# Weight transfers of 2 MB with rows of 16 KB for the two mixtures of a two-block layer stack

## The chip, the cores and the metric

The kernel runs on one core of a Trainium2 chip. The metric is the device time of one execution in microseconds (us). PE is the matrix engine, with its weight loads (PEld) listed apart; DVE and ACT are the vector and scalar engines, POOL is GpSimd, and SP is the engine whose queue issues the weight transfers. A transfer is carried out by 16 DMA engines: each moves the rows of eight partitions, and a row arrives as one packet. The time to tell apart from no change is about 0.2%.

## The reference

All is float32, for 256 tokens of width 1024. A first block (gated linear attention, three groups of dilated attention, a gated projection) ends in a mixture of 32 experts with hidden width 512, and every token goes to two of them. A second block runs two layers of mixing; the first has a dense feed-forward, the second a mixture of 8 experts with hidden width 2816, again two of them for each token. What matters here is the product of an expert:

```
def expert_block(args):                       # first mixture
    xb, e = args
    return (silu(xb @ w_gate[e]) * (xb @ w_up[e])) @ w_down[e]
...
for e in range(N_EXPERTS_2):                  # second mixture
    out = out + gate[..., e:e + 1] * swiglu(x, w1[e], w3[e], w2[e])
```

The weights of the first mixture are 192 MB, those of the second 264 MB. Every weight is read once.

## The kernel before

The program runs nine phases in a row: `b1` (first block), `moe1` (first mixture), `mix0`, `ffn0`, `ple0`, `mix1`, `ffn1` (second mixture, method `moe2`), `ple1` and `fin`. Weights come through one stream (`Stream`, L236 to 275) in the order of a plan that `Kern.plan` writes (L525). Each entry of the plan is a tile of 128 partitions by 2048 float32, which is 1 MB in rows of 8 KB.

A ring of three such tiles serves all phases (`RING`, L17). A phase may widen it by a pool of its own (`WIDE`, L23): 13 more tiles for `moe1`, opened already near the end of `b1`, and 6 more for `ffn1`, opened when that phase starts. `fill` (L255) issues the next entries as long as a tile is free: one of the wide pool if the entry belongs to the phase that opened it, else one of the ring. `get` (L268) hands the next tile to the consumer and gives back the one handed out before. In the program, then, the transfer of entry k+16 in `moe1`, and of entry k+9 in `ffn1`, waits until the readers of entry k are done. All these transfers are issued from SP's queue at L264, and they complete on eight semaphores in turn, so that a transfer also waits for the eighth before it to have landed.

In `moe1` (`experts1`, L1183) the loop over 8 groups of four experts has 8 steps for gate and up and 4 steps for down. A step takes two tiles, that is 2 MB, and runs eight products, four experts beside each other in strips of 32 columns of PE.

In `ffn1` (`moe2`, L1894) there are two halves of four experts. Each half has 11 groups of 8 steps (gate and up), then two rounds of 22 steps (down). A step (`tiles`, L1918) takes one tile of 1 MB: eight products read it directly; ACT copies three 512-column pieces of it, chosen at run time, into a buffer `fw` (two of these buffers, `FLEX`), and six smaller products read that.

In each mixture, after its first part of products, a branch tests whether an expert has overflowed its places; its body (`overflow`, L976) reads weights straight from memory by small transfers and is skipped for the inputs here.

Of the kernel before, what the change touches and what calls it, by code (L numbers as in the profile page):

```python
# [7 lines left out]
F32 = mybir.dt.float32  # L8
# [11 lines left out]
DIL = ((128, 1), (512, 4), (2048, 16))  # L20
NEG = -1e30

WIDE = {"b1": 0, "moe1": 13, "mix0": 0, "mix1": 0, "ffn0": 2, "ffn1": 6, "ple0": 4, "ple1": 4, "fin": 0}  # L23

SPLIT = 4
CAP1, CAP2 = 32, 64
# [3 lines left out]
ROUTED = {"moe1": ("wr", 36), "ffn1": ("wr2", 8)}  # L30
# [91 lines left out]
def prep(I):  # L122
    I = {k: np.asarray(v) for k, v in I.items()}
    A = {}
# [22 lines left out]
    w = I["w_in"][0]  # L147
# [15 lines left out]
    g = I["w_gate"][0].reshape(8, 4, 8, 128, 512).transpose(0, 2, 3, 1, 4)  # L163
    u = I["w_up"][0].reshape(8, 4, 8, 128, 512).transpose(0, 2, 3, 1, 4)
# [8 lines left out]
    for l in range(2):  # L173
        w = I["w_in_2"][l]
        rb, cb = 512, 1536
        q = cb + qperm
# [10 lines left out]
        w = I["w_out_2"][l][np.concatenate([rows_of[m][128 * j:128 * j + 128] for m, j in MIXED])]  # L187
        wo.append(np.stack([_kt(w[c:c + 512], 4) for c in (0, 512)]))
        w = I["ple_gate_w_2"][l]
# [19 lines left out]
    A["f13"] = w13(I["ffn_w1_2"], I["ffn_w3_2"])[0]  # L209
    A["f2"] = w2(I["ffn_w2_2"])[0]  # L210
    g, u = [I[n][0].reshape(2, 4, 8, 128, 11, 2, 4, 32).transpose(0, 4, 2, 3, 1, 6, 5, 7) for n in ("moe_w1_2", "moe_w3_2")]
    A["m13"] = np.stack([g, u], -3).reshape(2, 11, 8, 128, 4, 512)
    A["m2"] = I["moe_w2_2"][0].reshape(2, 4, 22, 128, 2, 512).transpose(0, 4, 2, 3, 1, 5)
    A = {k: np.ascontiguousarray(v) for k, v in A.items()}
    return A, dict(c0=o0, c1=o1, c2=o2, pv=opv, rows=orow, sm1=osm1, sm2=osm2)

# [2 lines left out]
class Bank:  # L219


    def __init__(self, k, t):
        self.k, self.t, self.q = k, t, set()
# [12 lines left out]
class Stream:  # L236

    def __init__(self, k, plan, base):  # L240
        self.k, self.plan, self.i, self.issued, self.tiles = k, plan, 0, 0, []
        self.pools, self.free, self.phase, self.last = [base], [RING], None, None

    def widen(self, pool, n, phase):
# [10 lines left out]
    def fill(self):  # L255
        while self.issued < len(self.plan):
            ph, src = self.plan[self.issued]
            c = [j for j in range(len(self.pools)) if self.free[j] and (j == 0 or ph == self.phase)]
            if not c:
                return  # L260
            j = c[-1]
            self.free[j] -= 1
            t = self.pools[j].tile([128, 2048], F32, name="w")
            self.k.nc.sync.dma_start(t[:, :src.shape[-1]], src)  # L264
            self.tiles.append((j, t))
            self.issued += 1
# [11 lines left out]
class Kern:  # L278
# [244 lines left out]


    def plan(self):  # L525
        A, p = self.A, []
        half = lambda ap: [ap[:, i * (ap.shape[-1] // 2):(i + 1) * (ap.shape[-1] // 2)] for i in range(2)]
        for ph in self.phases:
            l = int(ph[-1]) if ph[-1].isdigit() else 0
            q = []  # L530
            if ph == "b1":
                q += [A["wgv"]] + [A["wgh"][i] for i in range(4)] + [A["wdh"][i] for i in range(12)]
                q += [A["wb1"][i] for i in range(8)]
            if ph == "moe1":
                for g in range(8):
                    q += [A["wgu"][8 * g + k] for k in range(8)] + [A["wdn"][4 * g + k] for k in range(4)]
            if ph == f"mix{l}":
                q += [A["wz"][l, i] for i in range(4)] + [A[n][l] for n in ("wc", "wz5", "wz6")] + [A["wo"][l, i] for i in range(2)]
            if ph == "ffn0":
                for j in range(11):  # L540
                    q.append(A["f13"][j])
                    if j and j % 2 == 0:
                        q.append(A["f2"][:, (j // 2 - 1) * 4096:(j // 2) * 4096])
                q.append(A["f2"][:, 20480:])
            if ph == f"ple{l}":
                q += [A["wpp"][l]] + [A["wpg"][l, i] for i in range(2)]
            p += [(ph, h) for ap in q for h in half(ap)]
            if ph == "ffn1":
                for c in range(2):
                    p += [(ph, A["m13"][c, j, k].rearrange("p e d -> p (e d)")) for j in range(11) for k in range(8)]  # L550
                    p += [(ph, A["m2"][c, i, k].rearrange("p e d -> p (e d)")) for i in range(2) for k in range(22)]
        return p

    def run(self):
        tc, nc, A = self.tc, self.nc, self.A
        with ExitStack() as ctx:
            pool = lambda name, bufs=1, **kw: ctx.enter_context(tc.tile_pool(name=name, bufs=bufs, **kw))
            self.keep = pool("keep")
            ring = pool("ring", RING)
# [10 lines left out]
                setattr(self, n, self.keep.tile(list(A[n].shape), F32, name=n))  # L570
                q.dma_start(getattr(self, n), A[n])
            self.p = self.keep.tile([128, 2, S], F32, name="p")
            self.W = Stream(self, self.plan(), ring)
            self.W.fill()
            split = lambda pool, dt=F32R: [pool.tile([128, 8, S], dt, name="raw" + c, tag="raw" + c, bufs=1) for c in "hl"]
            self.split = lambda dt: split(self.keep, dt)
# [16 lines left out]
            def widen(ph):  # L593
                if WIDE.get(ph) and ph not in wider:
                    wider.add(ph)
                    pool = self.room.enter_context(tc.tile_pool(reuse_waits="tile", name="ring" + ph, bufs=WIDE[ph]))
                    self.W.widen(pool, WIDE[ph], ph)
            for i, ph in enumerate(self.phases):
# [12 lines left out]
                with self.room as c:  # L611
# [12 lines left out]
                    else:  # L624
                        self.final(x)
                if WIDE[ph]:
                    self.W.narrow()
# [1266 lines left out]
    def moe2(self, x):  # L1894
# [13 lines left out]
        with tc.tile_pool(reuse_waits="tile", name="m2", bufs=1) as pool:  # L1908
# [21 lines left out]
            def first_products(c, also):  # L1930
                g = [self.bank() for _ in range(3)]
                for k in range(8):
                    also(k)
                    tiles(g, [v[:, k] for v, _ in xg[c]], self.W.get().rearrange("p (e d) -> p e d", e=4), c)
                return g
            with tc.tile_pool(reuse_waits="tile", name="m2r", bufs=1) as rt:
# [86 lines left out]
                f = {}  # L2023
# [22 lines left out]
                        self.tick()  # L2046
                g0 = first_products(0, during)
                self.drain()
            m13 = self.A["m13"].rearrange("q j k p e d -> q j k p e d")
            m2 = self.A["m2"].rearrange("q f (j c) p e d -> q f j c p e d", c=2)  # L2050

            def units(first, unit):
                with tc.For_i(0, 2, 1) as q:
# [4 lines left out]
            one = lambda i: bass.ds(i, 1)  # L2058
            with tc.tile_pool(reuse_waits="tile", name="m2e", bufs=1) as work:
# [8 lines left out]
                def flush():  # L2068
                    while later:
                        later.pop(0)()  # L2070

                for c in range(2):
                    for j in range(11):
                        g = g0 if c == j == 0 else first_products(c, lambda k: flush() if k == 2 else None)
                        ts = []
                        for r in range(3):
                            t = work.tile([128, 256], F32, name="ft", bufs=4)
                            gu = g[r].t.rearrange("p (q a d) -> p q a d", a=2, d=64)
                            t4 = t.rearrange("p (q d) -> p q d", q=4)
                            for q, u in [(slice(0, 4), r)] if r < 2 else [(slice(b, b + 1), 2 + of_block[b]) for b in range(3)]:  # L2080
                                u = rsl[:, 5 * c + u:5 * c + u + 1]
                                self.act(t4[:, q], gu[:, q, 0], AF.Silu, scale=u)
                                nc.vector.scalar_tensor_tensor(t4[:, q], gu[:, q, 1], u, t4[:, q], op0=ALU.mult, op1=ALU.mult)
                            ts.append(t)

                        def post(j=j, ts=ts):

                            for r in range(3):
                                for s in range(4):
                                    for q in range(4 if r < 2 else 3):  # L2090
                                        i, f = place(s, q) if r == 2 else (0, q)
                                        o = 128 * r + 32 * (i if r == 2 else s)
                                        nc.vector.transpose(hT[32 * f:32 * f + 32, 2 * j:2 * j + 2, o:o + 32],  # L2093
                                                            ts[r][32 * s:32 * s + 32, 64 * q:64 * q + 64].rearrange(
                                                                "p (i d) -> p i d", i=2))
                        later.append(post)
                        if c == 0 and j == 5:
                            self.overflow(pool, x, ("g_ffn1", xs, lambda: None), rk, *f["over"], E, units,
                                          lambda i, k: m13[one(i[0]), one(i[1]), k, :, i[2]].rearrange("o u p d -> (o u p) d"),
                                          lambda i, c, f: m2[one(i[0]), f, one(i[1]), c, :, i[2]].rearrange("o u p d -> (o u p) d"),  # L2100
                                          lambda v: v.rearrange("p (q a i d) -> p q a i d", q=4, a=2, i=2))
                    if c:

# [1 line left out]
                    for d in range(2):  # L2105
                        g = [self.bank() for _ in range(3)]
                        for k in range(22):
                            w = self.W.get().rearrange("p (e d) -> p e d", e=4)
# [64 lines left out]
```

## Time and profile before

| | us |
|---|---|
| median of 3 runs | 2163.77 |
| lowest and highest run | 2163.45, 2166.29 |
| the profiled execution, its own time | 2167.51 |
| its span, to which all rows refer | 2165.9 |
| PE busy | 2016.7 (93%) |
| ACT busy | 1080.2 (50%) |
| DVE busy | 1060.6 (49%) |
| queue of the weights (q1), share of 16 engines | 71.1% |

The rows come from one profiled execution, which took 3.7 us more than the median. Times in the rows are us from the start of the span. In the page's 40 slices one slice is 54.1 us; a digit is a busy share in tenths. PE counts as busy while a product is in its pipeline, so its share does not tell whether it works at its peak. An fp32 product stands in the trace as two records.

### The profile page before, as it was taken

The page shows a single profiled execution, that of the slowest core. Times are in us where ns is not written, and L with a number is a line of the kernel's source. Part 1 is how long each engine was busy: PE and PEld are TensorE (multiplying, and loading weights), DVE is VectorE, ACT ScalarE, POOL GpSimd, SP SyncE. Part 2 cuts the span into 40 slices and gives each one's busy share as a digit, 9 for nine tenths or more (in the row PEclk, how much of TensorE's full clock was granted, in tenths as well). Part 3 has the DMA queues.
Part 4 walks back from the last instruction along what each step waited for, and adds up shares of the span by engine and source line. Part 5 has one row for each costly group of instructions (what it writes and reads, how often), then busy time and mean ns, then how long its engine had stood idle before and what let it go on. Part 6 is the DMA issues. An engine that isn't in the chain of part 4 may idle for free. (4 is left out here: it accounts for less than half of the span.)

```text
span 2165.9 us, 44126 instructions
## 1 busy us (share of the span) xinstructions
PE 2016.7 (93%) x17740; PEld 1461.7 (67%) x17740; DVE 1060.6 (49%) x2809; ACT 1080.2 (50%) x2178; POOL 18.7 (1%) x29
## 2 busy tenths in 40 slices
PE   7999998787877779999999999999899999999997
PEld 6999994222222248879999888866566756666746
DVE  5787653100100037777666787536655115566115
ACT  5566642000000025456456735457677777777775
POOL 0000000000000010000000100000000000000000
PEclk9999999899999999999999999889999999999998
DMA  5344597999999983316555331449999999999981
GB/s 179 120 146 149 175 376 305 418 420 420 419 420 420 419 343 109 109 61 216 179 193 191 114 128 52 175 159 396 399 410 418 416 405 407 418 418 417 418 351 47
DMA packets 88665, 613.73 MB, mean 283 GB/s; under 512 B 9879, under 2 KB 12071, under 8 KB 18560
## 3 DMA queue, kind: packets, MB, share of 16 engines
q1 hardware_dynamic: 86272, 604.74, 71.1%
q0 software_dynamic: 1344, 5.10, 0.7%
q8 instruction: 143, 2.34, 0.4%
q10 hardware_dynamic: 832, 0.94, 0.1%
q14 instruction: 74, 0.61, 0.1%
HBM read 609.69 MB, written 1.05 MB: 282 GB/s over the span
## 5 line engine op out<-in xcount | busy, mean ns | idle before, releaser
L314 ACT COPY fw<-w 128x512 f32 x792 | 439.0, 617 | 137.3 <-ACT fw L314 91.9
L341 ACT CAST wh<-w 128x512 fp32r<-128x512 f32 (+2 forms) x500 | 289.8, 585 | 293.8 <-PE ps L230 247.1
L342 DVE TENSOR_TENSOR wl<-w,wh 128x512 fp32r<-128x512 f32 (+2 forms) x500 | 317.9, 646 | 169.9 <-ACT wh L341 161.8
L230 PE MATMUL ps<-w,hT 128*32 128x512 f32 x1920 | 311.0, 597 | 31.4 <-DMA w<-wdn 26.0
L230 PE MATMUL ps<-rawh,wh 128*128 128x256 f32 x960 | 277.4, 289 | 1.1 <-ACT rawh L341 1.1
L230 PE MATMUL ps<-rawl,wh 128*128 128x256 f32 x960 | 271.0, 282 | 0.5 <-DVE rawl L342 0.5
L230 PE MATMUL ps<-rawh,wl 128*128 128x256 f32 x960 | 270.5, 282 | 0.0
L230 PE MATMUL ps<-fw,xg 128*32 128x384 f32 (+2 forms) x2112 | 252.8, 382 | 0.0
L230 PE MATMUL ps<-w,xg 128*32 128x512 f32 x1024 | 199.5, 600 | 43.2 <-DMA w<-wgu 43.0
L2093 DVE STREAM_TRANSPOSE hT<-ft 32x64 f32<-32x64 f32 x968 | 228.3, 236 | 16.3 <-DVEq L985 0.7
L230 PE MATMUL ps<-w,rawh 128*32 128x512 f32 x1408 | 206.2, 607 | 6.4 <-issue 6.4
L230 PE MATMUL ps<-w,rawl 128*32 128x512 f32 x1408 | 211.7, 593 | 0.0
L230 PEld LDWEIGHTS ps<-w,hT 128*32 128x32 f32 x1920 | 116.8, 110 | 135.6 <-DMA w<-wdn 64.0
L230 PEld LDWEIGHTS ps<-fw,xg 128*32 128x32 f32 x2112 | 137.8, 110 | 83.0 <-issue 24.0
L230 PEld LDWEIGHTS ps<-rawh,wh 128*128 128x128 f32 x960 | 181.8, 190 | 5.1 <-ACT rawh L341 1.6
L230 PEld LDWEIGHTS ps<-rawl,wh 128*128 128x128 f32 x960 | 181.9, 190 | 1.9 <-DVE rawl L342 0.7
L230 PEld LDWEIGHTS ps<-rawh,wl 128*128 128x128 f32 x960 | 181.9, 189 | 1.5 <-issue 0.9
L230 PEld LDWEIGHTS ps<-w,xg 128*32 128x32 f32 x1024 | 42.1, 109 | 185.7 <-DMA w<-wgu 111.7
L230 PEld LDWEIGHTS ps<-w,rawl 128*32 128x32 f32 x1408 | 105.2, 110 | 34.4 <-issue 0.9
L230 PE MATMUL ps<-hh,wh 128*128 128x256 f32 x416 | 124.4, 300 | 0.1
L230 PE MATMUL ps<-fw,hT 128*32 128x128 f32 (+2 forms) x1056 | 121.1, 380 | 0.5 <-ACT fw L314 0.3
L230 PE MATMUL ps<-hh,wl 128*128 128x256 f32 x416 | 116.2, 281 | 0.2 <-DVE wl L342 0.2
(520 smaller groups left out, 2983.7 us busy)
## 6 DMA issues: line engine op xcount, KB each, us to landing
w<-m SPq DMA_DIRECT2D x264, 1024.0 KB, 10.7
w<-wgu SPq DMA_DIRECT2D x128, 1024.0 KB, 19.9
w<-wdn SPq DMA_DIRECT2D x64, 1024.0 KB, 19.9
w<-f SPq DMA_DIRECT2D x32, 1024.0 KB, 5.1
w<-wz SPq DMA_DIRECT2D x20, 1024.0 KB, 5.5
w<-wdh SPq DMA_DIRECT2D x24, 768.0 KB, 4.3
w<-wb SPq DMA_DIRECT2D x16, 1024.0 KB, 5.6
w<-wo SPq DMA_DIRECT2D x8, 1024.0 KB, 5.1
```

The source lines that it names most:

```text
L230: return self.k.nc.tensor.matmul(out, lhsT, rhs, start=new, stop=stop, skip_group_check=True, **kw)
L314: self.nc.scalar.copy(out, in_)
L341: self.nc.scalar.copy(h, src)
L342: self.nc.vector.tensor_sub(l, src, h.bitcast(F32))
L2093: nc.vector.transpose(hT[32 * f:32 * f + 32, 2 * j:2 * j + 2, o:o + 32], ts[r][32 * s:32 * s + 32, 64 * q:64 * q + 64].rearrange("p (i d) ...
```

## The change

The two mixtures' weights are laid out in memory so that one transfer brings 2 MB in rows of 16 KB, and `WIDE` has 6 tiles of 2 MB for `moe1` and 3 for `ffn1`, in place of 13 and 6 of 1 MB. `plan` keeps entries of 1 MB, in pairs, and beside them a table `whole` with each pair's full source. `fill` takes a pair in one transfer when a wide tile is free. If none is free but two of the ring's tiles are, the pair goes there as two transfers of 1 MB in rows of 8 KB, as before. The first half of a wide tile gives nothing back when it has been read; the second half gives back the whole tile. The products, their operands and the small transfers of the overflow body compute the same from the new layout.

```
-WIDE = {"b1": 0, "moe1": 13, "mix0": 0, "mix1": 0, "ffn0": 2, "ffn1": 6, "ple0": 4, "ple1": 4, "fin": 0}
+WIDE = {"b1": 0, "moe1": 6, "mix0": 0, "mix1": 0, "ffn0": 2, "ffn1": 3, "ple0": 4, "ple1": 4, "fin": 0}
...
-    A["m13"] = np.stack([g, u], -3).reshape(2, 11, 8, 128, 4, 512)
-    A["m2"] = I["moe_w2_2"][0].reshape(2, 4, 22, 128, 2, 512).transpose(0, 4, 2, 3, 1, 5)
+    A["m13"] = np.stack([g, u], -3).reshape(2, 11, 4, 2, 128, 4, 512).transpose(0, 1, 2, 4, 3, 5, 6)
+    A["m2"] = I["moe_w2_2"][0].reshape(2, 4, 11, 2, 128, 2, 512).transpose(0, 5, 2, 4, 3, 1, 6)
...
     def fill(self):
         while self.issued < len(self.plan):
             ph, src = self.plan[self.issued]
-            c = [j for j in range(len(self.pools)) if self.free[j] and (j == 0 or ph == self.phase)]
-            if not c:
+            wide = len(self.pools) > 1 and self.free[1] and ph == self.phase
+            two = ph in ROUTED and not self.issued % 2
+            if two and wide:
+                self.free[1] -= 1
+                t = self.pools[1].tile([128, 4096], F32, name="w")
+                self.k.nc.sync.dma_start(t, self.whole[self.issued])
+                self.tiles += [(None, t[:, :2048]), (1, t[:, 2048:])]
+                self.issued += 2
+                continue
+            j = 1 if wide and ph not in ROUTED else 0
+            if self.free[j] < 1 + (two and j == 0):
                 return
-            j = c[-1]
             self.free[j] -= 1
...
             if ph == "ffn1":
                 for c in range(2):
-                    p += [(ph, A["m13"][c, j, k].rearrange("p e d -> p (e d)")) for j in range(11) for k in range(8)]
-                    p += [(ph, A["m2"][c, i, k].rearrange("p e d -> p (e d)")) for i in range(2) for k in range(22)]
-        return p
+                    q += [A["m13"][c, j, k].rearrange("p k e d -> p (k e d)") for j in range(11) for k in range(4)]
+                    q += [A["m2"][c, i, k].rearrange("p k e d -> p (k e d)") for i in range(2) for k in range(11)]
+            for ap in q:
+                if ph in ROUTED:
+                    whole[len(p)] = ap
+                p += [(ph, h) for h in half(ap)]
+        return p, whole
```

Two places show the order of SP's queue, in which each row is a kind of transfer with its tile's shape (128x2048 is 1 MB, 128x4096 is 2 MB). The first is the end of `b1` up to the branch of `moe1`; `wb` are the last weights of `b1`, `wgu` and `wdn` those of the mixture. Before:

```order
L264 DMA w<-wgu 128x2048
L264 DMA w<-wb 128x2048 x2
L264 DMA w<-wgu 128x2048 x3
L264 DMA w<-wb 128x2048
L264 DMA w<-wgu 128x2048 x10
L264 DMA w<-wdn 128x2048 x8
L264 DMA w<-wgu 128x2048 x15
L984 TENSOR_LOAD fi
```

After:

```order
L265 DMA w<-wgu 128x4096
L274 DMA w<-wb 128x2048 x2
L265 DMA w<-wgu 128x4096
L274 DMA w<-wb 128x2048
L265 DMA w<-wgu 128x4096 x3
L274 DMA w<-wgu 128x2048 x3
L265 DMA w<-wgu 128x4096
L265 DMA w<-wdn 128x4096 x4
L265 DMA w<-wgu 128x4096
L274 DMA w<-wgu 128x2048
L265 DMA w<-wgu 128x4096 x4
L997 TENSOR_LOAD fi
```

Before the first product of the mixture 16 MB can be on their way (13 wide tiles and the ring), and 23 MB follow ahead of the branch; now it is six wide tiles and the ring's three, 15 MB, and 21 MB follow.

The second place is SP's queue in `ffn1`, where before 51 and then 213 transfers of 1 MB of `m` stand in a row, each behind the readers of the ninth before it. Now, from the phase's start:

```order
L274 DMA w<-m 128x2048 x3
L265 DMA w<-m 128x4096 x3
L274 DMA w<-m 128x2048 x2
L265 DMA w<-m 128x4096 x3
L274 DMA w<-m 128x2048 x2
L265 DMA w<-m 128x4096 x3
```

Three transfers of 2 MB alternate with two of 1 MB, so a wide tile comes round every 8 MB. In the whole program 83 transfers of 2 MB and 26 of 1 MB carry the first mixture, 99 and 66 the second.

## Rows read from the trace of the kernel before

**Rows 1.** The page's 40 slices: PE, granted clock, DMA engines, GB/s.
```profile
PE   7999998787877779999999999999899999999997
PEclk9999999899999999999999999889999999999998
DMA  5344597999999983316555331449999999999981
GB/s 179 120 146 149 175 376 305 418 420 420 419 420 420 419 343 109 109 61 216 179 193 191 114 128 52 175 159 396 399 410 418 416 405 407 418 418 417 418 351 47
```
**Rows 2.** Who waited for whom, whole run, engine PE: total us, times, longest.
```profile
PE ps L230 <- DMA w<-wgu: 43.0, 71, 1.6
PE ps L230 <- DMA w<-wdn: 26.0, 39, 2.3
```
**Rows 3.** Stretches: length, busy us (records) of PE, PEld, DVE, ACT, POOL; clock; DMA share; GB/s.
```profile
440.00:780.00 340.00, 270.16 (x1263) 73.61 (x1261) 25.20 (x40) 14.56 (x24) 0.00 (x0) 1.00 1.01 420
1800.00:2040.00 240.00, 239.85 (x2753) 165.89 (x2749) 127.85 (x523) 179.33 (x349) 0.00 (x0) 1.00 1.01 418
```
**Rows 4.** PE's timeline, late in moe1: start, length, operation, count, idle before.
```profile
755.60 1.91 PE L230 MATMUL ps<-w,xg 128*32 128x512 f32 x8 [0.59 <-DMA w<-wgu]
...
768.07 1.91 PE L230 MATMUL ps<-w,xg 128*32 128x512 f32 x8 [0.58 <-DMA w<-wgu]
```
**Rows 5.** ACT's timeline in ffn1, behind the branch and late in the second half.
```profile
1571.56 1.66 ACT L314 COPY fw<-w 128x512 f32 x3 [0.70 <-ACT fw L314]
1573.92 1.66 ACT L314 COPY fw<-w 128x512 f32 x3 [0.70 <-ACT fw L314]
...
2036.47 1.66 ACT L314 COPY fw<-w 128x512 f32 x3 [0.72 <-PE ps L230]
2038.98 1.66 ACT L314 COPY fw<-w 128x512 f32 x3 [0.84 <-DMA w<-m]
2041.46 1.66 ACT L314 COPY fw<-w 128x512 f32 x3 [0.82 <-DMA w<-m]
```
**Rows 6.** L264's transfers issued from 1586 to 1600, us from issue to landing.
```profile
DMA to landing us min/median/max: 7.8/8.4/11.4
```
**Rows 7.** The same from 1676 to 1696.
```profile
DMA to landing us min/median/max: 11.8/12.8/15.1
```
**Rows 8.** The same from 1784 to 1800, and from 2005 to 2025.
```profile
DMA to landing us min/median/max: 6.6/7.3/8.6
...
DMA to landing us min/median/max: 13.7/14.5/17.3
```
**Rows 9.** DMA view, 1151.29 to 1151.91: 60 packets of 4 KB and one semaphore's.
```profile
DMA packets 61, 0.25 MB, mean 396 GB/s; under 512 B 1, under 2 KB 1, under 8 KB 61
q1 hardware_dynamic: 61, 0.25, 96.5%
```
**Rows 10.** DMA view, 117.53 to 119.02: packets of 6 KB alone.
```profile
q1 hardware_dynamic: 97, 0.60, 95.2%
```
**Rows 11.** DMA view, 1380.58 to 1382.56: packets of 8 KB alone.
```profile
q1 hardware_dynamic: 103, 0.84, 100.5%
```
**Rows 12.** DMA view, 1372.56 to 1372.86: semaphore packets alone.
```profile
q1 hardware_dynamic: 15, 0.00, 2.8%
```
**Rows 13.** SP's queue as moe1 begins: start, length of the run of issues, count.
```profile
300.68 16.14 SPq L264 DMA_DIRECT2D w<-wgu  x10
343.17 0.80 SPq L264 DMA_DIRECT2D w<-wdn  x2
```
**Rows 14.** PE's timeline behind the branch of moe1.
```profile
387.44 3.75 PE L230 MATMUL ps<-pw,ysg 128*128 128x256 f32 x8 [6.75 <-issue]
```
**Rows 15.** DMA view, 2125 to 2127: one 16 KB packet of the instruction queue.
```profile
q8 instruction: 1, 0.02, 2.8%
```

More of the change, by code (lines that the diff above doesn't have):

```diff
@@ L236, with __init__ @@
 class Stream:
-    def __init__(self, k, plan, base):
-        self.k, self.plan, self.i, self.issued, self.tiles = k, plan, 0, 0, []
+    def __init__(self, k, plan, whole, base):
+        self.k, self.plan, self.whole, self.i, self.issued, self.tiles = k, plan, whole, 0, 0, []
         self.pools, self.free, self.phase, self.last = [base], [RING], None, None
@@ L525, in plan @@
     def plan(self):
-        A, p = self.A, []
+        A, p, whole = self.A, [], {}
         half = lambda ap: [ap[:, i * (ap.shape[-1] // 2):(i + 1) * (ap.shape[-1] // 2)] for i in range(2)]
@@ L546, in plan @@
                 q += [A["wpp"][l]] + [A["wpg"][l, i] for i in range(2)]
-            p += [(ph, h) for ap in q for h in half(ap)]
             if ph == "ffn1":
                 for c in range(2):
-                    p += [(ph, A["m13"][c, j, k].rearrange("p e d -> p (e d)")) for j in range(11) for k in range(8)]
-                    p += [(ph, A["m2"][c, i, k].rearrange("p e d -> p (e d)")) for i in range(2) for k in range(22)]
-        return p
+                    q += [A["m13"][c, j, k].rearrange("p k e d -> p (k e d)") for j in range(11) for k in range(4)]
[5 more added lines that the diff above has]
+        return p, whole
     def run(self):
@@ L572, in run @@
             self.p = self.keep.tile([128, 2, S], F32, name="p")
-            self.W = Stream(self, self.plan(), ring)
+            self.W = Stream(self, *self.plan(), ring)
             self.W.fill()
@@ L2048, in moe2 @@
                 self.drain()
-            m13 = self.A["m13"].rearrange("q j k p e d -> q j k p e d")
-            m2 = self.A["m2"].rearrange("q f (j c) p e d -> q f j c p e d", c=2)
+            m13, m2 = self.A["m13"], self.A["m2"]
             def units(first, unit):
@@ L2098, in moe2 @@
                             self.overflow(pool, x, ("g_ffn1", xs, lambda: None), rk, *f["over"], E, units,
-                                          lambda i, k: m13[one(i[0]), one(i[1]), k, :, i[2]].rearrange("o u p d -> (o u p) d"),
-                                          lambda i, c, f: m2[one(i[0]), f, one(i[1]), c, :, i[2]].rearrange("o u p d -> (o u p) d"),
+                                          lambda i, k: m13[one(i[0]), one(i[1]), k // 2, :, k % 2, i[2]].rearrange("o u p d -> (o u p) d"),
+                                          lambda i, c, f: m2[one(i[0]), f, one(i[1]), :, c, i[2]].rearrange("o u p d -> (o u p) d"),
                                           lambda v: v.rearrange("p (q a i d) -> p q a i d", q=4, a=2, i=2))
```

## The prediction

> **What bounds the kernel now.** Read the page's slices first [rows 1]. Two long plateaus show the DMA engines at 9 of 10 and about 420 GB/s: one from the seventh to the fourteenth slice, the first mixture, and one from the twenty-seventh to the thirty-eighth, the second. Outside them the weights' queue has air, and the change touches no other transfer. Then read who waits inside each plateau.
>
> In the first mixture PE waits for weights: 71 times for `wgu` and 39 times for `wdn`, 69.0 us together [rows 2], and the timeline shows what that looks like. PE works 1.91 us, idles 0.59 us until the next megabyte lands, and starts again every 2.49 us (five such intervals in 12.47 us) [rows 4]. At 420 GB/s [rows 3] a megabyte takes 1,048,576 / 420,000 = 2.497 us. So this stage runs at the pace of the transfers. PE has a fifth of its time to spare there (270 of 340 us busy), and a faster PE would gain nothing.
>
> In the second mixture the transfers are as busy (418 GB/s, 2.51 us a megabyte), but PE is busy in 239.85 of 240 us [rows 3], and no wait of PE for `m` stands among its waits, where [rows 2] has the only two for a mixture's weights. PE's own pace shows in ACT's copies, three for each step: they start 2.36 us apart where nothing else is to do [rows 5]. So PE is the faster of the two by 0.15 us a step there, and lives on the lead that the nine tiles give. That lead is used up as the stage runs. The time from issue to landing grows from 8.4 to 12.8 us between 1586 and 1696 [rows 6, 7], PE's stops at the change of rounds refill it, and it grows again from 7.3 to 14.5 us [rows 8]. At the end of that second stretch ACT's copies wait for `w<-m` for the first time, at 2038.98 and 2041.46 [rows 5]. The lead is at zero there, and the wait has not yet reached PE. The stage is bound by PE with nothing to spare.
>
> **The change, part by part.**
>
> *A row of 16 KB instead of two of 8 KB.* Nowhere does the weights' queue move a 16 KB row, so its time is extrapolated from three sizes. Time per packet is share times 16 engines times the window, over the packets. At 4 KB: 0.965 x 16 x 620 ns = 9573 ns, less 9 for the semaphore's packet, over 60 = 159.4 ns [rows 9]. At 6 KB: 0.952 x 16 x 1490 / 97 = 234.0 ns [rows 10]. At 8 KB: 1.005 x 16 x 1980 / 103 = 309.1 ns [rows 11]. The steps of 2 KB cost 74.6 and 75.1 ns: a straight line, with 9.7 ns per packet that no byte explains. Four more such steps give 608.5 ns for 16 KB, against 618.2 for two packets of 8 KB. A transfer also ends in one packet of 9 ns on each engine, which counts up its semaphore: 0.028 x 16 x 300 / 15 [rows 12]. Per megabyte and engine that is 8 x 309.1 + 9 = 2481.8 ns before, and 4 x 608.5 + 4.5 = 2438.5 after, 43 ns less. The measured 2497 ns holds 15 ns more; if they too come per packet, half of them go, and the saving is 51 ns. I take 45 ns, 1.8%.
>
> [...]
>
> *The first mixture.* The last `wgu` ahead of the mixture is issued by 317 us, and the next transfer, 343.17, waits for PE's first step [rows 13]. From there to the end of the plateau the queue never runs dry, so the stage's end is that moment plus what is left to bring. Before, 16 MB are ahead and 176 MB are left. After, six wide tiles and the ring's three are ahead, 15 MB, and 177 MB are left: 1 MB more, +2.5 us. Of the 177, 77 transfers of 2 MB carry 154 MB in long rows (83 in all, six ahead), and 23 MB come through the ring as before. 154 x 45 ns = 6.9 us saved. Together -4.4 us. A step took two tiles of 1 MB and now takes one of 2 MB, so what PE waits for at each step, and at the last one, is the same 2 MB. Ahead of the branch SP's queue holds 21 MB, some 51 us of work from about 345; that covers to 397. PE stands still there for 6.75 us and goes on at 387.44 [rows 14], so I cost the branch at nothing; without the cover the stage would end later by what the queue ran dry.
>
> *The second mixture, lead.* PE-bound as it is, faster transfers gain nothing there by themselves. What the change takes away is lead. A wide tile goes back when both its halves are read, and is needed again six steps later, where a tile of 1 MB was needed eight steps after it went back. Two steps of 2.4 us, that is 4.8 us, are gone for the first half of each pair. What it gives is a slower loss of lead: three quarters of the bytes in long rows, 0.75 x 45 = 34 ns for each step. The first stretch, some 50 steps up to about 1700, ends now with about 2 us of lead (the longest landing in [rows 7] is 15.1 us, and in [rows 8] 17.3 us when the lead is gone). 2 - 4.8 + 50 x 0.034 = -1.1, so PE waits 1.1 us. The second, some 96 steps up to 2040, ends now at zero: 0 - 4.8 + 96 x 0.034 = -1.5, so it waits 1.5 us. Together +2.6 us, between 0 (if the small slack of ACT's two buffers hides it) and 5.
>
> [...]
>
> *The rest.* SP issues 83 + 26 + 99 + 66 = 274 transfers for the mixtures instead of 456, at 0.4 us each [rows 13] on a queue that waits most of the time: nothing. The scheduler puts some gathering products of `moe1` one step later on PE, beside steps that wait for transfers anyway: nothing.
>
> **Sum.** -4.4 + 2.6 = -1.8 us. From the profiled execution's 2167.5 that is 2165.7; that execution stands 3.7 us over the median, so against the runs' 2163.8 the forecast is **2162.0 us**. With the saving between 43 and 51 ns (-4.1 to -5.4 in the first mixture) and 0 to 5 us of waits, this case spans 2158.4 to 2164.7. It is 0.1% faster, less than the 0.2% (4.3 us) that a measurement can tell.
>
> **The rivals.**
>
> *Slower, the lead is too short.* PE waits for `m` in every stretch. For it: the lead is at zero already [rows 5], and a 2 MB tile needs some 2.5 us more to land. The price is 4.8 us at the start of the stage, before its branch, and in the two stretches above, if the transfers' gain gives none of it back: 14.4 us, less 4.4 gained in the first mixture, 2173.8; with 10 us of it, 2169.4. It decides from the point where the landing of a 2 MB tile takes longer than six steps of PE, 14.4 us. Against it: the faster stream shortens that landing as it goes.
>
> *It does not do what it says.* Long rows save little in the full stream. In the extreme a 16 KB row is moved as two packets of 8 KB; then only half of the semaphores' packets go, 4.5 ns x 154 = 0.7 us, against 2.5 us for the missing megabyte, and the lead in the second mixture is lost without relief (2.8 + 4.8 us): 2163.8 + 1.8 + 7.6 = 2173.2. With a third of my saving, 15 ns, it is +0.2 in the first mixture and 2.2 + 3.7 of waits in the second: 2169.9. [...] For it: 15 of the 2497 ns are not of the packets' own making. Against it: no row shows a 16 KB row of weights, but every size shown went as one packet, with the same 9.7 ns.
>
> *Faster, the stream gives back more.* By the slope of [rows 9 to 11] the bytes alone take 64 x 37.4 = 2397 ns a megabyte, so a full stream spends 100 ns on other things, of which I let 45 go. If 75 go, the first mixture saves 11.6 - 2.5 = 9.1 us, the second keeps its lead (56 ns a step, 5.4 us over 96 steps), and the time is 2154.7; with all 100, 2150.9. For it: packets in the full stream may wait for more than an idle one shows.
>
> *Long packets are slow.* The one kind of 16 KB packet in the trace, the instruction queue's, takes 0.028 x 16 x 2 us = 0.90 us [rows 15]. At that price 182 transfers of 8 packets per engine cost 0.29 x 8 x 182 = 420 us more, 2580. Against it: that queue brings code, not weights, and the line through three sizes bends nowhere.
>
> **How the numbers follow.** The forecast 0.48, more from the stream 0.24, short lead 0.13, little saved 0.12, slow packets 0.03. Faster by over 0.2% is under 2159.4: 0.24 and 0.06 of the forecast, 0.30. Slower is over 2168.1: 0.10 of the short lead, 0.11 of little saved and 0.03, 0.24. Within it, 0.46. The range runs from 2154, which leaves out the lower third of the faster case, to 2173, which leaves out the upper ends of the two slower ones and the last: about 0.18 outside.
>
> **What would show it.** Packets of 16 KB in the DMA view, 608 to 615 ns each; 427 to 428 GB/s in the middle of the first mixture instead of 420, and starts of PE's steps 4.9 us apart for 2 MB; the last `wdn` product 4 us earlier. In the second mixture waits of PE or of ACT's copies for `m` of a few us in all, near 1700 and from 1950 to 2040. It is wrong if the rate stays at 420 (no long packets), if the mixture's last step is not earlier, or if waits for `m` add up to more than 5 us.

## The result and the profile after

The changed kernel takes 2195.49 us (median of 4 runs, 2191.61 to 2197.43) against 2163.61 for the kernel before: a ratio of 1.0142 (95% interval 1.0125 to 1.0160), some 31 us slower (32 by the two medians). The forecast was 2162.0 with a range from 2154 to 2173. The profiled executions have spans of 2193.8 and 2165.9 us, 27.9 us apart; that is what the rows below have to explain.

Begin with the slices, to be held against [rows 1] (PE, granted clock, DMA engines, GB/s):

```profile
PE   7999997766666689999999999899799999999997
...
PEclk9999999887888899999999999799899999999998
DMA  5344597999999963235544431469899999999971
GB/s 177 118 144 154 179 378 304 425 425 425 428 425 426 424 268 124 78 122 189 180 159 176 134 116 61 173 262 410 340 423 423 407 380 384 391 387 385 416 315 51
```

The first plateau is at 425 and not at 420: the long rows do what they say. The second falls to 380 to 391 GB/s from slice 33 on, where it was 405 to 418. So the transfers are slower there, or somebody asks for them more slowly. The stretches tell (columns as in [rows 3]):

```profile
440.00:780.00 340.00, 217.37 (x1255) 62.38 (x1257) 25.02 (x40) 14.21 (x23) 2.58 (x5) 0.83 1.01 426
...
1800.00:2040.00 240.00, 225.30 (x2477) 145.70 (x2473) 132.78 (x535) 166.10 (x323) 0.00 (x0) 1.00 0.97 385
```

From 1800 to 2040 PE ran 2477 records where it had run 2753, and for 14.7 us it did nothing. PE's waits in a part of that stretch, 1800 to 1960 (total us, times, longest):

```profile
PE ps L230 <- ACT fw L324: 10.6, 16, 0.9
```

PE does not wait for `w<-m` here. It waits for ACT's copies, and the copies do not wait for their tile either: in steps 132 to 219 each tile had landed 3 to 14 us before its first copy began. What they wait for stands in the chain of waits from 1850 to 1900 (start, length, what held it up); ACT and DVE take turns between 1863 and 1868:

```profile
1863.12 0.48 ACT ft L313
1863.63 0.49 DVE ft L2095
1864.15 0.23 DVE hT L2105
1864.39 0.23 DVE hT L2105
1864.64 0.23 DVE hT L2105
...
1864.91 0.48 DVE ft L2095
...
1867.28 0.29 DVE ft L2095
1867.59 0.06 ACT ft L313
...
1867.81 0.62 ACT fw L324
```

This is the end of a group of eight gate and up steps. ACT takes the activation of five pieces of the group's sums into `ft`, and DVE multiplies each by its other half. The last three pieces share one tile, and there the rows show the activation of the fourth and of the fifth piece waiting until DVE is through with the piece before (in the next group for 1.29 us until 1888.02 and for 0.51 us until 1889.35). DVE also moves the finished `ft` into `hT` by 44 transposes of 0.24 us each. Here are the two queues at the end of the next group, first ACT and then DVE:

```profile
1881.75 1.66 ACT L324 COPY fw<-w 128x512 f32 x3 [0.71 <-PE ps L230]
1884.88 0.47 ACT L313 ACTIVATE ft<-ps,rsl 128x256 f32<-128x256 f32 x1 [1.47 <-PE ps L230]
1885.74 0.47 ACT L313 ACTIVATE ft<-ps,rsl 128x256 f32<-128x256 f32 x1 [0.38 <-PE ps L230]
1886.42 0.31 ACT L313 ACTIVATE ft<-ps,rsl 128x64 f32<-128x64 f32 x1 [0.21 <-PE ps L230]
1888.02 0.31 ACT L313 ACTIVATE ft<-ps,rsl 128x64 f32<-128x64 f32 x1 [1.29 <-DVE ft L2095]
1888.23 0.61 ACT L324 COPY fw<-w 128x512 f32 x1
```

```profile
1885.39 0.48 DVE L2095 SCALAR_TENSOR_TENSOR ft<-ps,rsl,ft 128x256 f32<-128x256 f32 x1 [8.68 <-ACT ft L313]
1885.91 0.73 DVE L2105 STREAM_TRANSPOSE hT<-ft 32x64 f32<-32x64 f32 x3
1886.67 0.48 DVE L2095 SCALAR_TENSOR_TENSOR ft<-ps,rsl,ft 128x256 f32<-128x256 f32 x1
1887.19 0.48 DVE L2105 STREAM_TRANSPOSE hT<-ft 32x64 f32<-32x64 f32 x2
1887.70 0.28 DVE L2095 SCALAR_TENSOR_TENSOR ft<-ps,rsl,ft 128x64 f32<-128x64 f32 x1
```

The first copy for the next group's first step (1888.23) stands behind the fourth `ft`, which waits 1.29 us for DVE; and DVE is late because three and then two transposes stand between its products. It is not the tile that the copy waits for, since that landed at 1881.82, 6.4 us ahead of it; four `ft` start in between, the last of them 0.21 us ahead of the copy.

In the kernel before, the order is another one. On ACT the first copy stands behind the third `ft`, two more behind the fourth, and the fifth `ft` comes after these; on DVE no transpose stands between the first and the second product, and only 1, 6 and 8 stand in between from then on. Its two queues at the end of a group, first ACT and then DVE, whose last row is the first product of the next group:

```profile
1855.02 0.31 ACT L303 ACTIVATE ft<-ps,rsl 128x64 f32<-128x64 f32 x1 [0.20 <-PE ps L230]
1855.23 0.61 ACT L314 COPY fw<-w 128x512 f32 x1
1855.74 0.32 ACT L303 ACTIVATE ft<-ps,rsl 128x64 f32<-128x64 f32 x1
1855.95 1.13 ACT L314 COPY fw<-w 128x512 f32 x2
1857.51 0.31 ACT L303 ACTIVATE ft<-ps,rsl 128x64 f32<-128x64 f32 x1 [0.43 <-DVE ft L2083]
```

```profile
1853.99 0.48 DVE L2083 SCALAR_TENSOR_TENSOR ft<-ps,rsl,ft 128x256 f32<-128x256 f32 x1 [6.42 <-ACT ft L303]
1854.85 0.48 DVE L2083 SCALAR_TENSOR_TENSOR ft<-ps,rsl,ft 128x256 f32<-128x256 f32 x1 [0.38 <-ACT ft L303]
1855.25 0.22 DVE L2093 STREAM_TRANSPOSE hT<-ft 32x64 f32<-32x64 f32 x1
1855.41 0.24 DVE L2083 SCALAR_TENSOR_TENSOR ft<-ps,rsl,ft 128x64 f32<-128x64 f32 x1
1855.68 1.48 DVE L2093 STREAM_TRANSPOSE hT<-ft 32x64 f32<-32x64 f32 x6
...
1873.54 0.48 DVE L2083 SCALAR_TENSOR_TENSOR ft<-ps,rsl,ft 128x256 f32<-128x256 f32 x1 [6.43 <-ACT ft L303]
```

A group took 19.5 us there (1853.99 to 1873.54) and takes 21.8 us now: DVE's first product of two groups in a row starts at 1863.63 and 1885.39.

The difference by parts of the second mixture, from the starts of ACT's first copy of each step (steps 0 to 263; us):

| steps | before | after | difference |
|---|---|---|---|
| 0 to 40, first half | 123.9 | 123.8 | 0 |
| 40 to 56, with the branch | 49.1 | 52.8 | +3.7 |
| 56 to 88, groups of the first half | 78.2 | 75.8 | -2.4 |
| 88 to 132, two rounds of down | 111.5 | 116.5 | +5.0 |
| 132 to 220, groups of the second half | 221.2 | 245.1 | +23.9 |
| 220 to 263, two rounds of down | 109.8 | 111.0 | +1.2 |
| 0 to 263 | 693.6 | 725.0 | +31.4 |

The mixture starts 3.4 us earlier than before, and with +31.4 that gives, to a tenth, the 27.9 us between the two spans. Three quarters of the loss lie in eleven groups.

### The profile page after: what moved, and what is told of

Read it like the earlier page. It is cut to its first block, busy times and chain, and to the rows that moved or that the text cites. A ratio compares the mean times of both kernels' runs of the same rounds, so it can differ in the third digit from the quotient of the medians.

```text
span 2193.8 us, 43786 instructions
## 1 busy us (share of the span) xinstructions
PE 1958.6 (89%) x17740; PEld 1428.7 (65%) x17740; DVE 1064.1 (49%) x2809; ACT 1082.1 (49%) x2178; POOL 18.6 (1%) x29
## 5 line engine op out<-in xcount | busy, mean ns | idle before, releaser
L230 PE MATMUL ps<-w,hT 128*32 128x512 f32 x1920 | 282.5, 645 | 46.6 <-DMA w<-wdn 42.4
L230 PE MATMUL ps<-fw,xg 128*32 128x384 f32 (+2 forms) x2112 | 235.7, 382 | 13.3 <-ACT fw L324 13.3
L230 PE MATMUL ps<-w,xg 128*32 128x512 f32 x1024 | 157.9, 710 | 90.3 <-DMA w<-wgu 90.3
L230 PE MATMUL ps<-w,rawh 128*32 128x512 f32 x1408 | 195.1, 607 | 12.3 <-DVEq L998 12.3
L230 PEld LDWEIGHTS ps<-w,hT 128*32 128x32 f32 x1920 | 101.1, 115 | 139.9 <-DMA w<-wdn 58.0
L230 PEld LDWEIGHTS ps<-w,xg 128*32 128x32 f32 x1024 | 32.8, 121 | 199.9 <-DMA w<-wgu 139.2
L2095 DVE SCALAR_TENSOR_TENSOR ft<-ps,rsl,ft 128x64 f32<-128x64 f32 (+1 forms) x110 | 39.8, 364 | 174.2 <-ACT ft L313 171.4
```

Of the source, the lines that this page charges most:

```text
L230: return self.k.nc.tensor.matmul(out, lhsT, rhs, start=new, stop=stop, skip_group_check=True, **kw)
```

## The experiments

Each kernel was timed beside the kernel before on its chip, whose median was 2166.0 to 2166.7 us beside the runs e1 to e10. "Group" is the time from one group to the next in the second half, "mixture" the time from step 0 to step 263 in the profiled execution (before: 19.5 and 693.6 us).

| run | median us | ratio to before (95%) | group | mixture |
|---|---|---|---|---|
| the change | 2195.49 | 1.0142 (1.0125 to 1.0160) | 21.8 | 725.0 |
| e1_after_pin | 2192.69 | 1.0129 (1.0108 to 1.0151) | 21.4 | 719.8 |
| e2_before_late | 2182.54 | 1.0071 (1.0052 to 1.0091) | 20.8 | 707.2 |
| e3_moe_long | 2164.63 | 0.9992 (0.9981 to 1.0003) | 19.5 | 694.4 |
| e4_halves | 2175.10 | 1.0038 (1.0026 to 1.0050) | 19.5 | 699.5 |
| e5_after_both | 2170.06 | 1.0022 (1.0007 to 1.0037) | 19.5 | 702.4 |
| e6_before_both | 2190.28 | 1.0113 (1.0086 to 1.0140) | 21.8 | 717.6 |
| e7_ffn_long | 2214.07 | 1.0220 (1.0192 to 1.0248) | 21.8 | 740.4 |
| e8_moe_long16 | 2160.85 | 0.9980 (0.9966 to 0.9994) | 19.5 | 693.5 |
| e9_after_three | 2166.80 | 0.9993 (0.9983 to 1.0003) | 19.6 | 693.9 |
| e10_moe16_behind | 2158.94 | 0.9966 (0.9952 to 0.9980) | 19.6 | 693.6 |

### ACT's order alone (e1_after_pin, e2_before_late)

In e1, the changed kernel, the fourth and fifth activation of a group are written between the next step's copies:

```
                 for f in range(3):
-                    self.cp(fw[:, f:f + 1], w[:, bass.ds(who[c][f], 1)])
+                    with self.after(last):
+                        i = (nc.cur_bb, self.cp(fw[:, f:f + 1], w[:, bass.ds(who[c][f], 1)]))
+                    if chain:
+                        last = hold.pop(0)(i) if f != 1 else i
```

> The changed kernel with one thing moved: in the second half of the second mixture (its eleven gate and up groups) ACT's queue is put back into the order that it has in the kernel before: after the third ft activation of a group one copy fw for the next group's first step, then the fourth ft, two copies, the fifth ft. Transfers, buffers and all else stay those of the changed kernel. Theory A (the compiler's new order on ACT costs the time: copies that PE waits for stand behind an ft that waits for DVE): those eleven groups take 29.2 us each as before and not 31.4, so 23.8 us come back, about 2171.5 us. Theory B (the three 2 MB buffers are too few, PE lives without a lead): order makes no difference, the time stays within 2190 to 2197 us.

In e2, the kernel before, the copies are held behind those activations:

```
                 for f in range(3):
-                    self.cp(fw[:, f:f + 1], w[:, bass.ds(who[c][f], 1)])
+                    with self.after(hold[min(f, 1)] if hold else None):
+                        self.cp(fw[:, f:f + 1], w[:, bass.ds(who[c][f], 1)])
+                hold.clear()
```

> The kernel before with one thing moved: in the second half of the second mixture ACT's queue gets the order of the changed kernel (the copies fw for the next group's first step behind the fourth ft activation, two of the three behind the fifth). All transfers stay at 1 MB through 13 and 6 buffers. Theory A (order on ACT): slower than before by 11 times about 2.2 us, 20 to 24 us, so 2184 to 2188 us. Theory B (too few buffers): nothing has been taken from the buffers, so 2163 to 2166 us.

Neither theory got what it wanted: e1's 2192.69 us lie in theory B's range, e2's 2182.54 in neither. (The expectation's groups of 29.2 and 31.4 us are wrong, they measure 19.5 and 21.8; the difference that it reckons with stands.) The late order costs the kernel before 1.3 us a group, so order does cost time with all the buffers in place, and theory B (too few buffers) had nothing for that. It is not ACT's order alone, since DVE's moved with it: in e2 0, 1, 4, 4 and 35 transposes stand behind the five products. And ACT's good order gives the changed kernel back only 0.4 us a group. DVE's queue in e1 shows why:

```profile
1884.27 0.28 DVE L2104 SCALAR_TENSOR_TENSOR ft<-ps,rsl,ft 128x64 f32<-128x64 f32 x1
1884.59 2.49 DVE L2119 STREAM_TRANSPOSE hT<-ft 32x64 f32<-32x64 f32 x10
1887.11 0.28 DVE L2104 SCALAR_TENSOR_TENSOR ft<-ps,rsl,ft 128x64 f32<-128x64 f32 x1
```

With ACT put in order, ten transposes stand between two of DVE's products. The `ft` that waits for the second product (1.50 us, until 1887.42) now stands ahead of ACT's copies, of which the next starts at 1887.64. Theory A fell in this form; the next one, A2, took both queues together.

### The same buffers with 1 MB transfers (e4_halves)

```
-                self.k.nc.sync.dma_start(t, self.whole[self.issued])
+                for i in range(2):
+                    self.k.nc.sync.dma_start(t[:, 2048 * i:2048 * i + 2048], self.plan[self.issued + i][1])
```

> The buffers of the changed kernel (6 and 3 of 2 MB, given back when both halves are read), each filled by two transfers of 1 MB with rows of 8 KB. ACT's queue has the order of the kernel before in the second half of the second mixture, and a mixed one in the first half. Theory A (order): no 23.8 us there; what is left is a megabyte less ahead of the first mixture (+2.5 us, no long rows to pay for it) and two steps less of lead in the second (0 to 10 us): 2166 to 2177 us. Theory B (2 MB buffers, too few of them): 2188 us or more, as the changed kernel or worse, since the rows are short again.

2175.1 us, in theory A's range, and groups of 19.5 us. With the buffers of the changed kernel and transfers of half the size, both queues have the order of the kernel before in the second half. So it is the size of one transfer, not the number of buffers, that moved the order there. At the second mixture's branch the size is not what moved it: there e4 has all 44 transposes ahead of the branch, as the changed kernel has, and PE stands still for 12.47 us. That is most of the +3.7 us in steps 40 to 56; its rounds of down take 1.4 us more in the first half and 1.0 in the second. The +5.8 us of this run's second mixture are therefore not the price of the buffers alone. From the first mixture's first product to its last landing it takes 454.0 us, against 450.1 before.

### Both queues (e5_after_both, e6_before_both)

In e5 each of the 44 transposes and five products of a group is written behind the one ahead of it, with the copies between the activations as in e1; e6 does the same to the kernel before with the changed kernel's order. The counts are the transposes behind each product:

```
+MOVES = (0, 1, 6, 8, 29)
...
+def next_on_dve(do):
+    with self.after(dve[0]):
+        dve[0] = (nc.cur_bb, do())
```

> The changed kernel, with both queues put back into the order of the kernel before in the eleven gate and up groups of the second mixture's second half: on ACT the copies fw for the next group between the third, fourth and fifth ft, on DVE the five products into ft with 0, 1, 6, 8 and 29 of the 44 transposes behind them (in the changed kernel 3, 2, 4, 4 and 31). Transfers of 2 MB and three buffers stay. Theory A2 (the two queues together make a chain ACT, DVE, ACT, and the copies stand in it): the groups go from 21.8 to 19.5 to 19.7 us, some 23 us come back, 2169 to 2173 us. Theory B2 (a 2 MB transfer itself slows these steps, whatever the order; the run with two transfers of 1 MB has 19.5 us a group): groups of 21 us or more, 2186 us or more.

> The kernel before, with both queues in the order of the changed kernel in the same eleven groups (on ACT the copies behind the fourth ft, on DVE 3, 2, 4, 4 and 31 transposes behind the five products). All transfers stay at 1 MB. Theory A2: 21.8 us a group and not 19.5, 22 to 25 us slower than before, 2187 to 2191 us. Theory B2: no more than the 1.3 us a group that ACT's order alone cost, 2180 to 2184 us.

Both came out as theory A2 said. The changed kernel with the old order falls by 25 us to 2170.1, and the kernel before with the new order rises to 2190.3. DVE's first product in two groups in a row, e5 and then e6:

```profile
1871.14 0.48 DVE L2141 SCALAR_TENSOR_TENSOR ft<-ps,rsl,ft 128x256 f32<-128x256 f32 x1 [6.43 <-ACT ft L313]
...
1890.70 0.48 DVE L2141 SCALAR_TENSOR_TENSOR ft<-ps,rsl,ft 128x256 f32<-128x256 f32 x1 [6.44 <-ACT ft L313]
```

```profile
1861.38 0.48 DVE L2129 SCALAR_TENSOR_TENSOR ft<-ps,rsl,ft 128x256 f32<-128x256 f32 x1 [8.70 <-ACT ft L303]
...
1883.14 0.48 DVE L2129 SCALAR_TENSOR_TENSOR ft<-ps,rsl,ft 128x256 f32<-128x256 f32 x1 [8.70 <-ACT ft L303]
```

19.56 and 21.76 us: the groups follow the order of the queues, with 2 MB transfers and with 1 MB ones. In e5 the first copy stands behind the third `ft` and waits for nobody:

```profile
1872.18 0.31 ACT L313 ACTIVATE ft<-ps,rsl 128x64 f32<-128x64 f32 x1 [0.20 <-PE ps L230]
1872.39 0.61 ACT L324 COPY fw<-w 128x512 f32 x1
1872.90 0.32 ACT L313 ACTIVATE ft<-ps,rsl 128x64 f32<-128x64 f32 x1
1873.10 1.14 ACT L324 COPY fw<-w 128x512 f32 x2
```

### One mixture at a time (e3_moe_long, e7_ffn_long, e8_moe_long16)

In e3 and e7 only one of the phases takes pairs, the other has its 1 MB tiles back; e8 is e3 with one tile of 1 MB more in the first mixture. Against the changed kernel:

```
-            two = ph in ROUTED and not self.issued % 2
+            two = ph in LONG and not self.issued % 2
```

> 2 MB transfers and six 2 MB buffers in the first mixture alone; the second mixture keeps 1 MB transfers and six buffers of 1 MB, and with them ACT's queue the order of the kernel before. Both theories: the first mixture ends as early as in the changed kernel, where the first copy of the second mixture starts 3.4 us earlier than before; nothing is lost after it. About 2160.4 us, 2159 to 2162. If instead the time is 2163 or more, the gain of the first mixture is given back by something that I have not seen.

> 2 MB transfers in the second mixture alone; the first mixture keeps 13 buffers of 1 MB. In the second half of the second mixture both queues have the order of the changed kernel; in the first half ACT has the copies behind all five ft. Theory A2: 21.8 us a group in the second half, and more than 19.5 in the first, 2190 to 2205 us. Theory B2: also slow in the second half; the first half then runs as in the changed kernel (18.9 us a group), 2190 to 2196 us.

> 2 MB transfers in the first mixture alone, and there one buffer of 1 MB beside the six of 2 MB, so that 16 MB are ahead of it as before, and all of the ring can be used. The second mixture as before. The first mixture has a megabyte less to bring than with six buffers alone: its last transfer lands 2.5 us earlier than there, 4.8 us earlier than before. 2159 to 2162 us when the phases between the mixtures hand that on; 2163 to 2166 if they take it back, as the run with six buffers had it.

e3's 2164.63 us lie above the range that was expected, and its 0.9992 holds both the 3.4 us and nothing, so by its time it decides little. Its first mixture takes 448.0 us as in the changed kernel (447.8), and yet its second mixture starts at 1407.9, only 0.3 us earlier than before. From the first mixture's last landing to the second mixture's first copy the profiled executions took between 611.0 (e5) and 619.4 us (e3; 617.6 before), so a few us at that point prove little by themselves. e7 lies above both theories' ranges and is worse than the whole change: in its first half ACT has the copies behind all five `ft`, and a group takes 23.8 us there (DVE's first products at 1605.91, 1629.58 and 1653.36). The second mixture's transfers are the same as in the changed kernel, and yet its first half has another order: the order hangs on things far away. e8 is a version that beats both kernels, by 0.20% (0.06 to 0.34): its first mixture takes 445.3 us from the first product to the last landing, where it took 450.1.

### The branch (e9_after_three, e10_moe16_behind)

At the second mixture's branch PE stands still for 12.29 us in the changed kernel and for 6.44 us before. Again it is DVE's queue: PE goes on at 1562.17, when DVE is through with the last of the transposes and has taken the branch (DVEq L998 in the row is DVE's sequencer at the branch). PE and then DVE, after:

```profile
1562.17 1.89 PE L230 MATMUL ps<-w,rawh 128*32 128x512 f32 x5 [12.29 <-DVEq L998]
```

```profile
1554.88 6.98 DVE L2105 STREAM_TRANSPOSE hT<-ft 32x64 f32<-32x64 f32 x28
```

In the kernel before, these 28 stand behind the branch. e9 and e10 hold all 44 back:

```
+                def flush_behind():
+                    i = nc.vector.tensor_copy(mark, seen[0][:1, 0, :1])
+                    with self.after((nc.cur_bb, i)):
+                        flush()
```

> The changed kernel with the two queues in the order of the kernel before in the eleven groups (as in the run before it that came to 2170 us), and one more thing moved: the 44 transposes of the group ahead of the second mixture's branch stand behind the branch on DVE. In the changed kernel all 44 stand ahead of it and PE stands still for 12.3 us there; in the kernel before 28 of them stand behind it and PE stands still for 6.4 us. Theory A3 (order on DVE again): PE's stop falls to 4 to 7 us, the eight steps around it from 34.0 to 26 to 28.5 us, and some 5 to 8 us come back: 2162 to 2166 us. Theory B3 (the buffers come back too late there, or the refill of the stream behind the branch is too slow): the stop may be shorter, but the steps behind it wait for m, and the time stays at 2168 to 2172 us.

> The kernel with 2 MB transfers in the first mixture alone and one 1 MB buffer beside its six (2160.9 us), with the 44 transposes ahead of the second mixture's branch moved behind it on DVE. The second mixture has 1 MB transfers and the order of the kernel before. PE's stop at the branch falls from 6.4 us to about 4, the stream starts again 2 to 3 us earlier behind it, and since the transfers set the pace from there on, that is what the end gains: 2157 to 2159 us. If PE sets it alone, the gain is lost in the same place: 2160 to 2162 us.

In e9 PE's stop is 6.72 us, the eight steps around it take 28.1 us and not 34.0 as in e5, and the second mixture takes 693.9 us: as long as before. (The median lies 0.8 us above theory A3's range and under B3's.) With the order of two queues mended in twelve places the change costs nothing, 0.9993 (0.9983 to 1.0003). PE's stop in e9:

```profile
1553.52 2.79 PE L230 MATMUL ps<-w,rawh 128*32 128x512 f32 x12 [6.72 <-issue]
```

e10's time is the best of all, 0.34% under before (0.20 to 0.48), but not for the reason given: its stop is 6.44 us as in e8, its second mixture takes the same 693.6 us, and the intervals of the two overlap. Where 28 transposes stood behind the branch already, moving the other 16 changed nothing. I take e8 and e10 for the same kernel, 0.2 to 0.35% faster than before.

## Why the prediction was wrong

**The step that failed is "The rest".** It let the compiler's new order pass with "nothing", having looked at PE and SP. The order had moved on ACT and DVE as well, in the second mixture, where PE is the bound with nothing to spare ([rows 3]) and where each of PE's steps waits for ACT's three copies. That term was not zero but +23.9 us in the eleven groups, and some 6 us at the branch (34.0 in e5, 28.1 in e9). Runs e5, e6 and e9 show both.

**The rival that looked right was not.** "Slower, the lead is too short" named a price of up to 14.4 us by waits for `m`. A reader who saw only the time would have taken this rival; e4, with the same three buffers, has groups of 19.5 us, and e5 has them with the 2 MB transfers too. The waits themselves did pass the 5 us that the prediction named as a sign of being wrong. In the changed kernel PE waits for `m` twice, 1.5 us in all, and ACT's copies 13 times, 19.4 us in all, where before they waited twice, 1.7 us. But all of these waits lie between 1538 and 1709, in the first half, and none in the eleven groups.

The waits cost most in the two rounds of down of the first half: between steps 90 and 109 the copies of seven of the eight pairs start 0.10 us behind their landing, and the 44 steps take 116.5 us and not 111.5. In e9, with the order mended, it is +4.5 us there and +1.9 in the last rounds. The forecast had 1.1 + 1.5 = 2.6, with 5 as the upper end: undersized by a factor of 2.5. Its two steps of lead are those by which a tile comes back too late; the 2.5 us more that a 2 MB tile needs to land, which this rival names, are not among them. e4, whose transfers bring one megabyte into the same buffers, loses only 1.4 and 1.0 us in these rounds. That fits, but does not prove it, since the order of e4's first half is another one.

e9 gains 2.0 us around the branch and 2.0 in the first half's groups, 18.9 us each where the copies happen to stand a step ahead. It also has 39.7 us for the first eight steps, as e1, e4 and e7 have, where the others have 41.8 to 42.4; what decides between the two is not shown. The three together hide the loss.

**The long rows.** Right, with a rate of 426 GB/s where 427 to 428 were forecast. Packets of 16 KB were forecast at 608 to 615 ns. From 1395.2 to 1399.4 there are 109 of them and 15 semaphore packets:

```profile
DMA packets 124, 1.79 MB, mean 425 GB/s; under 512 B 15, under 2 KB 15, under 8 KB 15
...
q1 hardware_dynamic: 124, 1.79, 99.3%
```

(0.993 x 16 x 4200 - 15 x 9) / 109 = 611 ns. Taking 8 x 74.85 = 598.8 ns for its bytes (16 KB in steps of 2 KB), 12 ns are left, near the 9.7 of the short packets.

**The first mixture.** Right in sign, half in size. 426 GB/s is 2.461 us a megabyte, 36 ns less than 2.497 where the forecast took 45, so 177 x 36 = 6.4 us less 2.5 for the megabyte that is not there ahead: -3.9. From the first product to the last landing the five executions with six 2 MB buffers took 447.8 to 448.8 us and the four with 1 MB tiles 450.1 to 450.8: -2.2 us, where -4.4 was forecast. 1.7 us of that stay open. e8 shows the price of the megabyte: with it the stage took 445.3 (444.4 in e10).

**PE's spare time there.** "A fifth" was too little. In the kernel before, PE started on a step's first megabyte and waited for the second (0.59 us a megabyte in [rows 4]), with two records under way at once (755.80 to 756.00); now the step's 2 MB land together and four are under way (750.10 to 750.30), 16 records (eight products) in the time that eight records took:

```profile
749.90 1.93 PE L230 MATMUL ps<-w,xg 128*32 128x512 f32 x16 [1.53 <-DMA w<-wgu]
...
765.43 3.40 PE L230 MATMUL ps<-w,xg 128*32 128x512 f32 x16 [3.71 <-DMA w<-wgu]
```

1.93 us for 2 MB, against 1.91 for 1 MB in [rows 4]. Busy time is not work, and a share of it is not a reserve.

**The sum.** Of its terms one figure is slightly off: 64 KB at the slope used come to 2395 ns and not 2397, on which nothing hangs. e9 measured -1.5 us (-3.7 to +0.6), and -1.8 was forecast for transfers and buffers. It agrees in part by luck: the first mixture gave less and the lead took more than forecast, and the first half's order and its first eight steps paid for the difference.

**What stays open.** Why the order moved. e4 shows that the size of one transfer did it in the second half. At the branch it is not that alone: e4 has PE's long stop with 1 MB transfers (12.47 us), and e7 with 2 MB ones in the second mixture does not have it (6.22). That the compiler reckons the end of a longer transfer later, and so lets an `ft` go ahead of the copy that reads that transfer, is only argued. Also open is what makes the stretch between the two mixtures vary by 8 us, and 1.7 us of the first mixture.

## What to carry to other kernels

Where a compiler sets the order of the queues, a change of transfers or buffers is also a change of order on engines that it never names: lay the queues of every engine of the stage that sets the end beside each other, before and after, down to ACT and DVE. An instruction that feeds the bound engine must not stand behind one that waits for a third engine (groups of 21.8 us here, and of 19.5 with the order mended in e5); when a tile has landed long before its reader starts, as here by 6.4 us, look at what stands ahead of the reader. And mend both queues of such a chain at once, since mending one let the other slide here (21.4 us a group in e1).

## What the runs showed of the hardware

PE's granted clock fell in the first mixture, from a mean of 1.00 between 440 and 780 [rows 3] to 0.83, with the same products and the same DMA share of 1.01. How PE works differs too: in that stretch it waited 39 times for `wgu`, 81.9 us in all and 3.9 us at the longest, where before it had waited 70 times, 42.5 us in all and 1.6 us at the longest. Whether these waits lowered the clock is not shown. Rows of 16 records at 1.93 us and at 3.40 us stand side by side above, with a granted clock of 1.00 over the first (749.90 to 751.80) and 0.56 over the second (765.40 to 768.85). The lower mean shows in every run with 2 MB transfers in the first mixture: their profiled executions have a mean clock of 0.943 to 0.954, the others 0.970 to 0.976. It cost little, since the transfers set the pace there: the stage's last product ends 1.0 us earlier than before, while its last transfer lands 2.3 us earlier.
